# Differential attention on one core: transposes and value products further behind the scores, row products and gated steps at other places

## The chip, the cores and the metric

One core of a Trainium2 chip runs the whole program. The time is device microseconds of one execution; the number before is the median of three runs. An execution's own trace has the profiled times. Engines are called PE (TensorE matmuls), PEld (its weight loads), DVE (VectorE), ACT (ScalarE), POOL (GpSimd) and SP (SyncE, which issues the weight DMAs).

## The reference, cut to what matters

256 tokens of width 1024 pass two transformer layers and a third block (gated linear attention, block attention, a feed-forward of width 4096). The first layer is differential attention: 8 heads with two score maps each over 512 keys (256 of a context, 256 of the tokens).

```python
def diff_softmax_mix(q, k, v, lam):
    s = jnp.einsum('bqhmd,bkhmd->bhmqk', q * (HEAD_DIM ** -0.5), k).astype(jnp.float32)
    p = jax.nn.softmax(s, axis=-1)
    a = p[:, :, 0] - lam * p[:, :, 1]
    return jnp.einsum('bhqk,bkhe->bqhe', a.astype(v.dtype), v)

def diff_head_out(o, subln_g, lam_init, w_o):
    of = o.astype(jnp.float32)
    of = of * lax.rsqrt(jnp.mean(of * of, axis=-1, keepdims=True) + LN_EPS) * subln_g * (1.0 - lam_init)
    return of.astype(o.dtype).reshape(B, Q, V_WIDTH) @ w_o
```

Queries and latent keys get a rotary embedding first. Each layer is modulated by rows computed from a condition vector c (`m = silu(c) @ w_mod + b_mod`, 48 column blocks for each of two layers), and ends in layer norms and a gated feed-forward (`swiglu`).

## The kernel before, in words

**Weights as a stream.** All weights come as 426 blocks of 128 x 1024 fp32 in the order of `make_plan` (L82). `Stream` (L242) keeps 11 raw blocks ahead by DMA (`dma`, L251, on SP's queue). Emitting an item (`emit`, L265) means one of three things. A "w" block is split into a high and a low fp32r part: ACT copies hi (L285), DVE subtracts lo (L291), and a matmul by it is three fp32r matmuls (`mmN` L357, `mmK` L380, `mmK_tail` L394). A few blocks stay raw and are used as fp32 (`get32`); of the output projection WO these are keys 4 to 7. An "m" block is a row product on DVE (L269): a 128 x 1024 block times the condition row, summed into one column of `mc`. Up to 8 split blocks are alive.

**When items are emitted.** `done` (L336) tells that a block is used up, and `pump` (L307) then emits what follows, at most one m a call, unless `hold` is set; `step(n)` (L319) emits up to n items at a given place, but no split beyond 7 alive; `get` and `mods` emit until a given item is there. So the plan's order and these calls place every split and row product in the queues of ACT and DVE, which run in program order.

**K, Q and V.** K is projected first. The loop at L616 does Q in 8 blocks (12 matmuls of 512 columns each) and puts between them the transposes of the roped and plain keys (`k_transposes` L598): kt3 behind Q2, ktc[0] behind Q3, kt2 behind Q5, ktc[1] behind Q6. The rope of a 128 x 1024 tile (L578) is four DVE operations on each half. kt2 is roped on DVE behind Q3's items, from two "mm" PSUM tiles, which the first V projection needs again. `v_proj(0, tt)` (L631) makes the first half of the values in four pieces, with the ropes of q and `st.step(2)` between them; the second half, `v_proj(1, tt)`, lies within the attention loop at rounds VAT = (0, 3, 6, 9).

**The attention loop** (L801). 16 items (token tile t, head h), one a round. Round i issues for item i `at_scores` (L656: two matmuls into one of two "big" PSUM tiles, DVE reduce to the negative maxima at L666, two exponentials on ACT at L667 and L668 with their sums), for item i-1 `at_mix` (L671: reciprocal, a small product, then p0 + coefficient x p1 at L675), for item i-2 `at_tr` (L677: four PE transposes into a "tr" tile, an ACT copy), for item i-3 `at_av` (L686: eight matmul instructions by the values and a square on ACT). After four heads `at_norm` and `at_norm2` normalize the group (DVE, with a power on POOL between), and `tr_half` (L719), five rounds behind the group's last scores, transposes it: ACT writes the high part, DVE the low one, or ACT alone where it stays fp32. `st.step(ATS[i])` emits two items in rounds 0 to 8 and one in rounds 9 to 20. From round 16 on `wo0` (L761) does output rows of the first token tile as WOK lists them. `load_x` and `scale_x` bring the residual and scale it on ACT (L799) in rounds 14 and 15.

**After it.** `linK8` (L914) finishes the output projection with the layer norm of tile 0 inside it; `ffn` (L942) runs six chunks, each with G, U, transposes (`tr`) and O products, the latter one chunk behind. Its `mid` callbacks make rows from columns (`col_row` L767: two sets of four PE transposes, two ACT copies). In the third block `steps` (L1526) places the gated linear attention's small pieces between projections: `g_z`, `g_b`, `g_kl`, `g_qk` and others, by round.

Of the kernel before, what the change touches and what calls it, by code (L numbers as in the profile page):

```python
# [40 lines left out]
NV = 5  # L41
NB = 17
XL = 9
W0 = 4
W1 = 64
# [6 lines left out]
WOK = {0: (0,), 1: (1, 2), 2: (3, 4), 3: (5, 6, 7)}  # L52
ATS = (2,) * 9 + (1,) * 12
VAT = (0, 3, 6, 9)
TK = 2
# [10 lines left out]
VM = (1, 1, 1, 1, 0, 0, 0, 0)  # L66
# [105 lines left out]
def body(ctx: ExitStack, tc: tile.TileContext, wst, prm, cst, cst2, poolp, xT_d, cT_d, x_d, head, lam_d,  # L172
# [443 lines left out]
    for k in range(KD):  # L616
# [5 lines left out]
        if k == 3:  # L622
            kt2 = rope(two(kps[2]), 0)
            k_transposes(ktc[0], 0)
        if k == 5:
            k_transposes(kt2, 2)
        if k == 6:
            k_transposes(ktc[1], 1)
    qr = {}

    def v_proj(c, tt):  # L631
# [5 lines left out]
        mmN(ps, lh, mkey(("V", c), 4))  # L637
        if tt == 3:
            st.hold = c == 1
            st.done(*mkey(("V", c), 4))  # L640
        A.activation(vv[:, tt, c * 512:(c + 1) * 512], ps, AF.Copy)

    for tt in range(4):
        v_proj(0, tt)
        st.step(TK)
        if tt < 2:
            qr[tt] = rope([(qps[tt], 0, 1024)], tt)
        else:
            q_transposes(qr[tt - 2], tt - 2)
    a1.close()  # L650
# [3 lines left out]
    ss, ssum, ops, state, osb, rr = {}, {}, {}, {}, {}, {}  # L654

    def at_scores(t, h):  # L656
        g = (t, h // 4)
        if h % 4 == 0:
            ssum[g] = small(4)
        sm = small(8)  # L660
        pr = [a2.t([P, 512], "p0", bufs=4), a2.t([P, 512], "p1", bufs=2)]
# [4 lines left out]
        V.tensor_reduce(sm[:, 0:2], ps, AX.X, OP.max, negate=True)  # L666
        A.activation(pr[0], ps[:, 0], AF.Exp, bias=sm[:, 0:1], accum_out=ssum[g][:, h % 4:h % 4 + 1])  # L667
        A.activation(pr[1], ps[:, 1], AF.Exp, bias=sm[:, 1:2], accum_out=sm[:, 2:3])  # L668
        state[t, h] = pr, sm, ssum[g][:, h % 4:h % 4 + 1]

    def at_mix(t, h):  # L671
        pr, sm, s0 = state[t, h]
        V.reciprocal(sm[:, 4:5], sm[:, 2:3])
        V.scalar_tensor_tensor(sm[:, 5:6], sm[:, 4:5], nlam, s0, op0=OP.mult, op1=OP.mult)
        V.scalar_tensor_tensor(pr[0], pr[1], sm[:, 5:6], pr[0], op0=OP.mult, op1=OP.add)  # L675

    def at_tr(t, h):  # L677
        pr = state.pop((t, h))[0]
        ps = trt()
        for j in range(4):  # L680
            TE.transpose(ps[:, j * P:(j + 1) * P], pr[0][:, j * P:(j + 1) * P], ident)
        aT = a2.t([P, 512], "aT", bufs=2)
        A.activation(aT, ps, AF.Copy)
        state[t, h] = aT

    def at_av(t, h):  # L686
        aT = state.pop((t, h))
# [1096 lines left out]
```

## Time and profile before

| | |
|---|---|
| median of 3 runs | 1149.41 us (1147.62 to 1149.92) |
| the profiled execution's own time | 1149.09 us |
| its span | 1147.2 us |
| mean granted clock of PE | 0.996 |
| busy share PE, PEld, DVE, ACT | 97%, 77%, 66%, 49% |

Times in the rows count from the span's first instruction. A row's duration for a matmul is modelled and overlaps the next, so the work of PE is read from one start to the next. "[0.98 <-DVE tok L592]" says how long the engine was idle before the row and what ended that.

### The profile page before, as it was taken

What the parts mean: (1) busy time and instruction counts of PE and PEld (TensorE: products, weight loads), DVE (VectorE), ACT (ScalarE), POOL (GpSimd) and SP (SyncE); (2) the same over time, 40 slices, a digit from 0 to 9 for tenths busy, and PEclk for the clock granted to TensorE, in tenths of its full rate; (3) what the DMA queues carried; (4) which work ended last, traced back from release to release, by engine and by line L of the source; (5) the groups of instructions that cost most, each with busy time, mean ns of one, the idle gap of its engine ahead of it and who ended that gap; (6) DMA issues with size and microseconds to landing.
All of it is one profiled execution on the core that took longest, in us unless ns stands there. A gap on an engine that the chain in (4) does not pass through costs nothing.

```text
span 1147.2 us, 14156 instructions
## 1 busy us (share of the span) xinstructions
PE 1110.0 (97%) x5186; PEld 880.4 (77%) x5186; DVE 759.9 (66%) x1114; ACT 557.4 (49%) x913; POOL 22.6 (2%) x35
## 2 busy tenths in 40 slices
PE   7999888999999999999999999999999999999998
PEld 3578665678888776888888688887778877888887
DVE  7984967669986865577455865545636776555465
ACT  3452456454444427534443765557226355445353
POOL 0000000000000000000000110000000000000000
PEclk9999999999999999999999999999999999999999
DMA  9973741569997926568464654553434646464611
GB/s 360 359 261 116 275 147 60 195 233 372 343 419 280 332 79 220 191 215 303 168 225 146 224 196 147 189 193 126 169 108 146 208 147 210 162 212 164 207 38 37
DMA packets 65922, 234.62 MB, mean 205 GB/s; under 512 B 7323, under 2 KB 8347, under 8 KB 65852
## 3 DMA queue, kind: packets, MB, share of 16 engines
q1 hardware_dynamic: 64080, 227.97, 55.9%
q10 hardware_dynamic: 1772, 5.74, 1.5%
q8 instruction: 41, 0.67, 0.2%
q14 instruction: 29, 0.24, 0.1%
HBM read 232.63 MB, written 1.05 MB: 204 GB/s over the span
## 4 chain that ended last, share of the span: by engine, by line
PE 79%; DVE 10%; ACT 4%; issue 3%; DMA 2%; POOL 0%; SPq 0%; ACTq 0%; POOLq 0%; DVEq 0%
PE mm L378 16%; PE mm L376 16%; PE mm L377 16%; PE big L390 12%; PE big L392 6%; DVE lo L291 3%; DMA raw<-in_dram 2%; DVE junkb L526 2%; DVE raw L269 1%; PE big L384 1%; DVE st L666 1%; PE big L404 1%; PE big L405 1%; PE big L403 1%; PE tr L981 1%
## 5 line engine op out<-in xcount | busy, mean ns | idle before, releaser
L291 DVE TENSOR_TENSOR lo<-raw,hi 128x1024 fp32r<-128x1024 f32 x316 | 374.5, 1221 | 133.1 <-ACT hi L285 129.6
L285 ACT ACTIVATE hi<-raw 128x1024 fp32r<-128x1024 f32 x316 | 321.5, 1056 | 70.7 <-PE mm L378 52.2
L376 PE MATMUL mm<-hi,xTh 128*128 128x512 f32 (+1 forms) x872 | 337.6, 387 | 2.8 <-ACT xTh L425 2.7
L377 PE MATMUL mm<-lo,xTh 128*128 128x512 f32 (+1 forms) x872 | 331.8, 380 | 2.0 <-DVE lo L291 1.3
L378 PE MATMUL mm<-hi,xTl 128*128 128x512 f32 (+1 forms) x872 | 332.2, 381 | 0.6 <-DVE xTl L738 0.4
L376 PEld LDWEIGHTS mm<-hi,xTh 128*128 128x128 f32 x872 | 164.1, 188 | 38.4 <-ACT xTh L425 4.6
L378 PEld LDWEIGHTS mm<-hi,xTl 128*128 128x128 f32 x872 | 164.0, 188 | 34.1 <-DVE xTl L426 1.9
L377 PEld LDWEIGHTS mm<-lo,xTh 128*128 128x128 f32 x872 | 164.2, 188 | 33.4 <-DVE lo L291 3.6
L269 DVE SCALAR_TENSOR_TENSOR raw<-raw,crow 128x1024 f32<-128x1024 f32 x80 | 96.8, 1219 | 0.0
L390 PE MATMUL big<-hi,hh 128*128 128x512 f32 x256 | 80.6, 396 | 0.0
L390 PE MATMUL big<-lo,hh 128*128 128x512 f32 x256 | 79.2, 391 | 0.0
L392 PE MATMUL big<-hi,hl 128*128 128x512 f32 x256 | 79.0, 390 | 0.0
L425 ACT ACTIVATE hh<-tr 128x512 fp32r<-128x512 f32 (+1 forms) x40 | 22.9, 575 | 89.6 <-PE tr L981 49.2
L961 ACT ACTIVATE h<-mm 128x512 f32<-128x512 f32 (+1 forms) x24 | 13.5, 561 | 91.6 <-PE mm L378 91.6
L392 PEld LDWEIGHTS big<-hi,hl 128*128 128x128 f32 x256 | 48.0, 188 | 10.3
L390 PEld LDWEIGHTS big<-lo,hh 128*128 128x128 f32 x256 | 48.0, 188 | 10.3
L426 DVE TENSOR_TENSOR hl<-tr,hh 128x512 fp32r<-128x512 f32 (+1 forms) x40 | 26.3, 662 | 44.0 <-ACT hh L425 43.2
L390 PEld LDWEIGHTS big<-hi,hh 128*128 128x128 f32 x256 | 46.7, 188 | 8.6
L420 POOL TENSOR_TENSOR st<-st,half 128x4 f32<-128x4 f32 (+1 forms) x28 | 21.7, 776 | 1029.0 <-DVE st L418 1015.9
L1607 DVE TENSOR_TENSOR h<-h 128x512 f32<-128x512 f32 x16 | 11.0, 689 | 33.8 <-ACT h L1606 33.7
L1606 ACT ACTIVATE h<-mm 128x512 f32<-128x512 f32 x16 | 9.6, 598 | 39.8 <-PE mm L378 39.8
L667 ACT ACTIVATE p<-big,st 128x512 f32<-128x512 f32 x16 | 11.0, 689 | 31.4 <-DVE st L666 31.4
(316 smaller groups left out, 1256.2 us busy)
## 6 DMA issues: line engine op xcount, KB each, us to landing
raw<-in_dram SPq DMA_DIRECT2D x426, 512.0 KB, 5.0
row<-in_dram ACTq DMA_DIRECT2D x8, 512.0 KB, 6.2
tok<-in_dram SPq DMA_DIRECT2D x8, 256.0 KB, 8.0
xa<-in_dram SPq DMA_DIRECT2D x2, 512.0 KB, 6.6
out_dram<-sg SPq DMA_DIRECT2D x3, 256.0 KB, 2.0
pmat<-in_dram ACTq DMA_DIRECT2D x1, 544.0 KB
crow<-in_dram ACTq DMA_DIRECT2D x1, 512.0 KB, 6.4
out_dram<-sg SPq DMA_DIRECT2D x2, 128.0 KB, 1.7
```

What stands on the lines that cost most here:

```text
L269: V.scalar_tensor_tensor(raw, raw, 1.0, crow, op0=OP.mult, op1=OP.mult, accum_out=mc[l][:, nb:nb + 1])
L285: A.activation(hi, raw, AF.Copy)
L291: V.tensor_tensor(lo, raw, hi.bitcast(F32), op=OP.subtract)
L376: TE.matmul(ps, h, hi[:, sl], start=s, stop=False)
L377: TE.matmul(ps, h, lo[:, sl], start=False, stop=False)
L378: TE.matmul(ps, l, hi[:, sl], start=False, stop=e)
L390: TE.matmul(halves[f], h, w[:, f * 512:(f + 1) * 512], start=first and b == 0, stop=False)
L392: TE.matmul(halves[f], l, hi[:, f * 512:(f + 1) * 512], start=False, stop=last)
L420: G.tensor_tensor(r, v, half_e[:, :w], op=OP.pow)
L425: A.activation(dh, ps, AF.Copy)
L426: V.tensor_tensor(dl, ps, dh.bitcast(F32), op=OP.subtract)
L526: V.scalar_tensor_tensor(junk, raws[b], 1.0, crow if s_ else ccrow, op0=OP.mult, op1=OP.mult, accum_out=acc[2 * s_ + b])
```

## The change

In the plan five more row products come ahead of the second half of V (NV, NB, VM), and those woven into the first feed-forward start three blocks later (W0, W1). In the Q loop ktc[0] goes behind Q4, ktc[1] stays behind Q6 and kt2 goes behind the first V projection. The four pieces of V emit 2, 2, 2 and 1 items, behind the rope or the transposes, and the stream is held from the fourth on. In the attention loop the mix, the transposes, the products and the group's steps lie one round further behind the scores; the exponentials are issued behind the transposes of an older item; the small division is done for two heads at once in even rounds; the squares of three groups are one ACT pass and one DVE reduce; gated steps come only in rounds 0, 2, 6, 10, 16, 17 and 18; V and the output rows move. Four further places change behind the loop. Removed bodies that stand above are left out.

```diff
-NV = 5
-NB = 17
+NV = 10
+NB = 12
 XL = 9
-W0 = 4
-W1 = 64
+W0 = 7
+W1 = 67
...
-WOK = {0: (0,), 1: (1, 2), 2: (3, 4), 3: (5, 6, 7)}
-ATS = (2,) * 9 + (1,) * 12
-VAT = (0, 3, 6, 9)
-TK = 2
+WOK = {0: (0, 1), 1: (2, 3), 3: (4, 5, 6, 7)}
+ATS = {0: 3, 2: 4, 6: 4, 10: 4, 16: 2, 17: 7, 18: 1}
+VAT = (0, 2, 6, 10)
+TK = (2, 2, 2, 1)
...
-VM = (1, 1, 1, 1, 0, 0, 0, 0)
+VM = (1, 1, 1, 6, 0, 0, 0, 0)
...
             kt2 = rope(two(kps[2]), 0)
-            k_transposes(ktc[0], 0)
-        if k == 5:
-            k_transposes(kt2, 2)
-        if k == 6:
-            k_transposes(ktc[1], 1)
+        if k in (4, 6):
+            k_transposes(ktc[k // 2 - 2], k // 2 - 2)
...
         mmN(ps, lh, mkey(("V", c), 4))
+        A.activation(vv[:, tt, c * 512:(c + 1) * 512], ps, AF.Copy)
         if tt == 3:
-            st.hold = c == 1
+            st.hold = True
             st.done(*mkey(("V", c), 4))
-        A.activation(vv[:, tt, c * 512:(c + 1) * 512], ps, AF.Copy)
 
     for tt in range(4):
         v_proj(0, tt)
-        st.step(TK)
         if tt < 2:
             qr[tt] = rope([(qps[tt], 0, 1024)], tt)
         else:
             q_transposes(qr[tt - 2], tt - 2)
+        if tt == 0:
+            k_transposes(kt2, 2)
+        st.step(TK[tt])
...
+        V.tensor_reduce(sm[:, 2 * (i % 2):2 * (i % 2) + 2], ps, AX.X, OP.max, negate=True)
+        state[i] = ps
+
+    def at_exp(i):
...
+        pr = [a2.t([P, 512], "p0", bufs=4), a2.t([P, 512], "p1", bufs=3)]
+        A.activation(pr[0], ps[:, 0], AF.Exp, bias=sm[:, 2 * o_:2 * o_ + 1],
+                     accum_out=ssum[t, h // 4][:, h % 4:h % 4 + 1])
+        A.activation(pr[1], ps[:, 1], AF.Exp, bias=sm[:, 2 * o_ + 1:2 * o_ + 2], accum_out=sm[:, 4 + o_:5 + o_])
+        state[i] = pr
+
+    def at_small(i):
+        t, h = items[i]
+        sm = pairs[i // 2]
+        V.reciprocal(sm[:, 6:8], sm[:, 4:6])
+        V.scalar_tensor_tensor(sm[:, 6:8], sm[:, 6:8], nlam, ssum[t, h // 4][:, h % 4:h % 4 + 2],
+                               op0=OP.mult, op1=OP.mult)
+
+    def at_mix(i):
+        pr = state[i]
+        V.scalar_tensor_tensor(pr[0], pr[1], pairs[i // 2][:, 6 + i % 2:7 + i % 2], pr[0], op0=OP.mult, op1=OP.add)
+        state[i] = pr[0]
...
-        jk = a2.t([P, P], "jk", bufs=2)
-        A.activation(jk, ps, AF.Square, accum_out=ss[g][:, h % 4:h % 4 + 1])
+        if g == (1, 1):
+            A.activation(a2.t([P, P], "jk1"), ps, AF.Square, accum_out=ss[g][:, h % 4:h % 4 + 1])
+        elif h % 4 == 3:
+            sq[g] = a2.t([P, 512], "jk")
+            A.activation(sq[g], ops[g], AF.Square)
 
     def at_norm(g):
...
+        v, r = small(4), small(4)
+        if g in sq:
+            V.tensor_reduce(ss[g], sq.pop(g).rearrange("p (h d) -> p h d", d=P), AX.X, OP.add)
+        V.scalar_tensor_tensor(v, ssum[g], LN_EPS, ssum[g], op0=OP.mult, op1=OP.mult)
+        V.scalar_tensor_tensor(v, ss[g], 1.0 / 128, v, op0=OP.mult, op1=OP.add)
+        G.tensor_tensor(r, v, half_e[:, :4], op=OP.pow)
+        rr[g] = r
...
+    def at_half(n):
+        t, f = items[n][0], items[n][1] // 4
+        tr_half(osb[t, f], f, t, xTh, xTl, scalars=sub, f32=f in WOF)
+
+    for i in range(n_it + 4):
+        g5, g6, g7 = [items[i - n] if n <= i < n_it + n and (i - n) % 4 == 3 else None for n in (5, 6, 7)]
+        last = i == n_it + 3
...
+        if i == n_it:
             g1c = mcol(0, 2)
...
         if i < n_it:
+            at_scores(i)
+        if 3 <= i < n_it + 3:
+            at_tr(i - 3)
+        if i < n_it:
+            at_exp(i)
+        if g7:
+            at_half(i - 7)
+        if i >= 4:
+            at_av(i - 4)
+        if i % 2 == 0 and 2 <= i < n_it + 2:
+            at_small(i - 2)
+        if 2 <= i < n_it + 2:
+            at_mix(i - 2)
+        if g6:
+            at_norm2((g6[0], g6[1] // 4))
+        if g5:
+            at_norm((g5[0], g5[1] // 4))
+        if last:
+            at_norm((1, 1))
+        st.step(ATS.get(i, 0))
         for tt in range(4):
             if VAT[tt] == i:
                 v_proj(1, tt)
         if i - n_it in WOK:
             wo0(WOK[i - n_it])
...
+        if i == n_it + 2:
+            col_row(g1c, s[1])
+        if last:
+            at_norm2((1, 1))
+            at_half(n_it - 1)
...
             st.done((name, k))
-        if name == "WO":
-            keep(KW["c"])
+            if name == "WO" and k == 3:
+                st.hold = True
...
-                if (j, 0) in mid:
-                    mid[j, 0]()
                 o(j - 1, 0, False)
-                if (j, 1) in mid:
-                    mid[j, 1]()
...
-            ln_core(t, ps, cur["grow"])
+            ln_core(t, ps, cur["grow"], lambda: st.step(2 * t))
...
     def wo_mid():
         cur["cols"] = mod_cols(0, 1, 0)
-
-    def wo_t0():
         cur["rows"] = ln_rows(0, ALPHA)
-        x_t(0)()
+
+    wo_t0 = x_t(0)
...
     def mid_gbr():
-        nx["G"] = col_row(nx["gb"][0])
+        nx["G"], nx["B"] = col_row(nx["gb"][0]), col_row(nx["gb"][1])
+        cur["grow"] = col_row(nx["g1p"])
         nx["cols"] = mod_cols(1, 1, 2)
-
-    def mid_br():
-        nx["B"] = col_row(nx["gb"][1])
-
-    def mid_pr():
-        cur["grow"] = col_row(nx["g1p"])
...
-    steps = [lambda: (g_z(0), g_z(1)), lambda: (g_b(0), g_b(1)), lambda: (g_kl(0), g_kl(1)), lambda: g_qk(0),
+    steps = [lambda: (g_z(0), g_z(1)), lambda: g_b(0), lambda: (g_b(1), g_kl(0)), lambda: (g_kl(1), g_qk(0)),
              lambda: g_qk(1), lambda: (g_a(0), g_a(1)), lambda: g_kv(0)]
```

## Rows read from the trace of the kernel before

**Rows 1.** The page, part 1: busy time of each engine.

```profile
PE 1110.0 (97%) x5186; PEld 880.4 (77%) x5186; DVE 759.9 (66%) x1114; ACT 557.4 (49%) x913; POOL 22.6 (2%) x35
```

**Rows 2.** Two stretches by windows: length, busy of PE, PEld, DVE, ACT, POOL, granted clock, DMA, GB/s.

```profile
118.00:212.00 94.00, 81.41 (x418) 55.70 (x417) 69.47 (x139) 49.58 (x132) 4.05 (x4) 0.98 0.46 156
83.00:90.00 7.00, 4.65 (x18) 3.73 (x18) 6.93 (x11) 2.14 (x3) 0.00 (x0) 0.76 0.92 355
```

**Rows 3.** What PE's weight loads waited for, 110 to 215: total, times, longest (us).

```profile
PEld tr L681 <- issue: 15.1, 9, 4.5
```

**Rows 4.** Timeline of PE in the Q stage: start, duration (us), engine, line, operation.

```profile
82.55 0.61 PE L392 MATMUL big<-hi,xTl 128*128 128x512 f32 x2
...
86.14 1.08 PE L602 MATMUL tr<-cst,tok 128*128 128x128 f32 x4 [1.36 <-DVE tok L592]
86.88 1.20 PE L390 MATMUL big<-hi,xTh 128*128 128x512 f32 x2
...
89.36 0.62 PE L390 MATMUL big<-hi,xTh 128*128 128x512 f32 x2
```

**Rows 5.** Timeline of DVE in the Q stage: the last step of the rope of kt2.

```profile
85.30 0.69 DVE L592 TENSOR_TENSOR tok<-tok,ropeb 128x512 f32<-128x512 f32 x1
```

**Rows 6.** Timeline of PE in the attention loop.

```profile
117.99 1.13 PE L665 MATMUL big<-kT,qz 64*128 64x512 f32 x4
...
124.71 1.99 PE L665 MATMUL big<-kT,qz 64*128 64x512 f32 x8
128.32 0.63 PE L681 MATMUL tr<-cst,p 128*128 128x128 f32 x4 [1.63 <-issue]
...
151.17 1.06 PE L694 MATMUL mm<-vv,aT 128*128 128x128 f32 x8
152.16 1.13 PE L665 MATMUL big<-kT,qz 64*128 64x512 f32 x4
153.22 0.66 PE L681 MATMUL tr<-cst,p 128*128 128x128 f32 x4
153.71 1.06 PE L694 MATMUL mm<-vv,aT 128*128 128x128 f32 x8
...
159.51 0.63 PE L681 MATMUL tr<-cst,p 128*128 128x128 f32 x4 [3.68 <-DVE st L707]
160.53 1.89 PE L694 MATMUL mm<-vv,aT 128*128 128x128 f32 x8 [0.40 <-ACT jk L696]
...
211.64 0.60 PE L722 MATMUL tr<-cst,osb 128*128 128x128 f32 x4
```

**Rows 7.** Timeline of PE among the output rows.

```profile
198.90 0.62 PE L390 MATMUL big<-hi,xTh 128*128 128x512 f32 x2
...
200.29 0.60 PE L681 MATMUL tr<-cst,p 128*128 128x128 f32 x4
...
206.49 5.32 PE L384 MATMUL big<-raw,pw 128*128 128x512 f32 x12
```

**Rows 8.** Groups of DVE and ACT by line, 118 to 212: count, busy, mean ns, idle before.

```profile
L269 DVE SCALAR_TENSOR_TENSOR raw<-raw,crow 128x1024 f32<-128x1024 f32 x17 | 20.1, 1219 | 0.0
L666 DVE TENSOR_REDUCE st<-big 128x2 f32<-128x1024 f32 x16 | 19.5, 1218 | 0.9 <-PE big L665 0.9
L675 DVE SCALAR_TENSOR_TENSOR p<-p,st,p 128x512 f32<-128x512 f32 x16 | 12.0, 752 | 0.6
...
L667 ACT ACTIVATE p<-big,st 128x512 f32<-128x512 f32 x16 | 11.0, 689 | 31.4 <-DVE st L666 31.4
```

**Rows 9.** Timeline of PE at the end of the first feed-forward layer.

```profile
391.54 1.04 PE L774 MATMUL tr<-cst,Gc 128*128 128x128 f32 x8
...
409.06 0.62 PE L390 MATMUL big<-hi,hh 128*128 128x512 f32 x2
```

**Rows 10.** Timeline of DVE at the same place.

```profile
400.95 0.68 DVE L426 TENSOR_TENSOR hl<-tr,hh 128x512 fp32r<-128x512 f32 x1
```

**Rows 11.** What PE waited for, 770 to 830.

```profile
PE tr L1447 <- DVE la L1442: 1.0, 1, 1.0
```

More of the change, by code (lines that the diff above doesn't have):

```diff
@@ L649, in body, with at_scores @@
             q_transposes(qr[tt - 2], tt - 2)
+        if tt == 0:
+            k_transposes(kt2, 2)
+        st.step(TK[tt])
     a1.close()
     a2 = Pool("a2")
-    ss, ssum, ops, state, osb, rr = {}, {}, {}, {}, {}, {}
-    def at_scores(t, h):
-        g = (t, h // 4)
+    ss, ssum, ops, state, osb, rr, pairs, sq = {}, {}, {}, {}, {}, {}, {}, {}
+    def at_scores(i):
+        t, h = items[i]
         if h % 4 == 0:
-            ssum[g] = small(4)
-        sm = small(8)
-        pr = [a2.t([P, 512], "p0", bufs=4), a2.t([P, 512], "p1", bufs=2)]
+            ssum[t, h // 4] = small(4)
+        if i % 2 == 0:
+            pairs[i // 2] = small(8)
+        sm = pairs[i // 2]
         ps = big().rearrange("p (m k) -> p m k", m=2)
@@ L665, in at_scores, with at_tr, at_av @@
             TE.matmul(ps[:, m], qz[d, h, t * P:(t + 1) * P], kT[d, h, :], start=True, stop=True)
[L666 to L678, printed above, removed]
+        V.tensor_reduce(sm[:, 2 * (i % 2):2 * (i % 2) + 2], ps, AX.X, OP.max, negate=True)
+        state[i] = ps
+    def at_exp(i):
+        t, h = items[i]
+        ps, sm, o_ = state.pop(i), pairs[i // 2], i % 2
+        pr = [a2.t([P, 512], "p0", bufs=4), a2.t([P, 512], "p1", bufs=3)]
[4 more added lines that the diff above has]
+    def at_small(i):
+        t, h = items[i]
+        sm = pairs[i // 2]
+        V.reciprocal(sm[:, 6:8], sm[:, 4:6])
[5 more added lines that the diff above has]
+        state[i] = pr[0]
+    def at_tr(i):
+        p0 = state.pop(i)
         ps = trt()
         for j in range(4):
-            TE.transpose(ps[:, j * P:(j + 1) * P], pr[0][:, j * P:(j + 1) * P], ident)
+            TE.transpose(ps[:, j * P:(j + 1) * P], p0[:, j * P:(j + 1) * P], ident)
         aT = a2.t([P, 512], "aT", bufs=2)
         A.activation(aT, ps, AF.Copy)
-        state[t, h] = aT
-    def at_av(t, h):
-        aT = state.pop((t, h))
+        state[i] = aT
+    def at_av(i):
+        t, h = items[i]
+        aT = state.pop(i)
         g = (t, h // 4)
@@ L799, in scale_x @@
         A.activation(xa[t], xa[t], AF.Copy, scale=ALPHA)
-    for i in range(n_it + 5):
+    def at_half(n):
[4 more added lines that the diff above has]
+        last = i == n_it + 3
         if i == XL:
@@ L823, in body @@
             wo0(WOK[i - n_it])
-        if 2 <= i <= n_it + 1:
-            at_tr(*items[i - 2])
-        st.step(ATS[i])
-        if 3 <= i <= n_it + 2:
-            t, h = items[i - 3]
-            at_av(t, h)
-            if h % 4 == 3:
-                at_norm((t, h // 4))
-        if i >= 5 and items[i - 5][1] % 4 == 3:
-            t, f = items[i - 5][0], items[i - 5][1] // 4
-            tr_half(osb[t, f], f, t, xTh, xTl, scalars=sub, f32=f in WOF)
+        if i == n_it + 2:
[3 more added lines that the diff above has]
+            at_half(n_it - 1)
     st.hold = False
@@ L1149, in ple @@
             A.activation(pw[t][:, f * 512:(f + 1) * 512], pst[f], AF.Copy)
-    ffn(0, fp, x_t(1), ac0(0), mid_pool, ac0(1), {XM: mid_xa, 2: mid_g2c, 3: mid_g2r, 4: mid_gb, 5: mid_gbr, (5, 0): mid_br, (5, 1): mid_pr})
+    ffn(0, fp, x_t(1), ac0(0), mid_pool, ac0(1), {XM: mid_xa, 2: mid_g2c, 3: mid_g2r, 4: mid_gb, 5: mid_gbr})
     pps = [big()]
```

20 lines of the change are left out of this document (1 added, 19 removed).

## Prediction

> **What bounds the kernel now.** I read the page's first part, then the two stretches by windows, then the waits of TensorE's weight loads, then the timelines of TensorE (PE), VectorE (DVE) and ScalarE (ACT) around each edit. PE is recorded busy for 97% of the span [rows 1], so nothing an edit does to DVE or ACT counts unless it fills a hole on PE, and the sum below is a sum of holes. The attention loop is where they are: between 118 and 212 us PE is busy 81.4 of 94.0 us [rows 2], so 12.6 us are idle by record. In the Q stage the stretch 83 to 90 us has 4.65 of 7.0 us busy at a granted clock of 0.76 [rows 2]. The weight loads that wait in the attention are mainly those of L681, the transposes of the mixed scores: 15.1 us in nine waits [rows 3]. They stand in PE's queue two rounds behind their scores and ahead of everything else, and a score has to pass reduce, exponentials and mix on DVE and ACT first.
>
> [...]
>
> **Work in the attention, by the starts of rows.** A value product takes 0.99 us (151.17 to 152.16), a pair of scores 1.06, four transposes 0.49 (153.22 to 153.71), so a round has 2.54 us of PE work [rows 6]; 16 rounds are 40.6. A V projection takes 124.71 - 117.99 less its scores' 1.06 = 5.66; four are 22.6. Output rows: 1.39 us for a split key (198.90 to 200.29), 1.72 for an fp32 one (5.15 for three from 206.49) [rows 6, 7]; four of each are 12.5. Four group transposes and one row from a column (two sets of transposes) are six times 0.49 = 2.9. Sum 78.6 us, against 117.99 to 211.64 + 0.49 = 94.1. So 15.5 us are idle or at the low clock.
>
> **The change, part by part.** All against the profiled execution, 1149.1 us (its span of 1147.2 and 1.9 around it), which is 0.3 us below the median of the runs shown.
>
> *Q stage.* The transposes of kt2 stand between Q5 and Q6. PE finishes Q5 at 82.55 + 0.45 = 83.0 and starts Q6 at 86.88, held by the rope on DVE that ends at 85.99 [rows 4, 5]. Of these 3.9 us the eight transposes are 0.98; 2.9 are waiting. Q6 then runs slowly: 2.48 us from 86.88 to 89.36 where three pairs cost 3 x 0.455 = 1.37 at full clock, 1.1 lost. The change puts these transposes behind the first V projection, 5.66 us of PE work later than now plus Q6 and Q7; the rope doesn't move. So the wait goes whole: **-4.0 us** (bounds -2.9, if the clock falls elsewhere, to -4.0). Late next would be the accumulators that the same rope releases for the first V projection; PE gets there near 89, three us after the rope's end. The other k transposes only change places among ready ones. Three row products move from behind V's blocks into Q5 to Q7, where DVE has nothing that PE awaits, and the V1 blocks are split after the second q rope; their first reader is the projection behind the first scores, some ten us later.
>
> *Attention.* The loop goes from mix at one round, transposes at two and products at three behind the scores to two, three and four; the gated steps go from one or two in every round to bursts ahead of the V projections (3, 4, 4, 4) and of the output rows; the small divisions are done for two heads at once; the squares for three of four groups in one ACT pass and one DVE reduce. DVE's prices: reduce 1.22, mix 0.75, row product 1.22 [rows 8], some 0.08 less from start to start; a split I take like a row product, one pass over a tile of the same size. DVE has about 2.0 us a round for scores, less than PE's 2.54, so without bursts PE leads. In a V round PE has 8.2 us and DVE 2.0 + 4 x 1.14 = 6.6. Before, 17 row products lay in this stretch [rows 8] and six more queued just ahead of the first reduce; now 14 do. I walked through the rounds with these prices, each engine in its queue order. What is left: round 4, transposes wait 1.5 us, since round 3's reduce and mix queue behind the burst of round 2; round 10 0.5, the transposes of the first head whose mix follows a group's norm; round 12 1.0, after round 10's burst, which also holds the low half of the transposed group; round 15 3.0, where ACT does a scale of x before each of two copies, the high half of the group's transposes comes behind the exponentials, its low half blocks DVE, and the pair's division and mix stand behind that. Sum 6.0; I add 0.8 for hand-overs. Of 15.5 us 6.8 stay: **-8.7 us**. Bounds: all gone -15.5; none +0 (the lockstep rival goes beyond). The burst ahead of the output rows lies beside 8 split and fp32 keys of matmuls; the last group's norm lies beside four fp32 keys (6.9 us), where before only three were left.
>
> *New waits, clock.* A wait of about 3 us costs more than itself: after the 3.7 us wait at 159.51 the product took 1.89 us by record against 1.06, and the Q stage above lost 1.1 at the lower clock. After 1.63 us at 128.32 the transposes took 0.63, as unhindered ones (0.66) [rows 6]. I expect two new waits of 3 us (round 15 and the one below) and take half of 1.1 for each: **+1.1** (0 to +2.2).
>
> *Feed-forward tail of the first layer.* Three rows are made from columns in one place instead of three, and eight row products start three blocks later. DVE had seven items between the last U and the low half of the first transposes (hl), which started at 400.95 [rows 10]; by the new plan there are ten, one of them the last O block, so hl starts 3 x 1.14 = 3.4 later and is ready at 405.0. On PE: from 391.54 [rows 9] seven sets of transposes at 0.49 (ACT's copies as fast, an estimate), 395.0; the first O product, 24 matmuls as in a V projection, 5.6, 400.6; transposes 0.5; then the last O product, whose third matmul needs hl: 3.5 us of waiting, then 22 of 24 matmuls, 5.0, end 410.0 against 409.06: **+1.0** (bounds -2.5, DVE not late, to +1.0).
>
> *GLA.* g_b(1) no longer follows g_b(0) at once; the wait of 1.0 us on la goes [rows 11], and one of the later sets may wait for a PSUM slot: **-0.7** (0 to -1.0).
>
> *At nothing.* The hold at the third output row and the step inside the normalization change no order: rows 4 to 7 are fp32 and release no slot, and at the step the splits stand at their limit. The two row loads move ahead of the normalization on ACT's queue; PE has the whole second half of the output product there, and if that cover were gone it would be a fraction of a us. Two row products leave that place for later ones in a stretch where DVE isn't awaited.
>
> Sum: -4.0 - 8.7 + 1.1 + 1.0 - 0.7 = -11.3, so **1137.8 us**.
>
> **Rivals.**
> *The waits nearly all go.* ACT and DVE keep up and 2 us stay: 4.8 less, 1.1 of clock less, 1131.9. For it: PE work exceeds DVE's in every kind of round. Against: bursts of four on an engine with one queue.
> *DVE still sets the pace.* Each burst and each group's norm puts the chain one step back and 11.5 us stay: 4.7 more, 1142.5. For it: DVE is busy 69.5 of 94 us now [rows 2], and 80 us would hold almost as much.
> *Every wait brings the low clock.* If all four of my residual waits were followed by 1.1 us of loss, 3.3 more, 1141.1. For it: the slow product behind 159.51; against it the one behind 128.32 [rows 6]. [...]
> *The Q wait only moves*, to the first V projection: 4.0 more, 1141.8. The rope's end at 85.99 speaks against it.
> *Lockstep, slower than before.* In every pair of rounds DVE's division waits for the second head's exponentials on ACT, and next round's reduce, from which the next exponentials come, stands behind it. A pair then costs two reduces, one set of exponentials, the division, two mixes and a pair of scores: 2.44 + 1.45 + 0.45 + 1.5 + 1.06 = 6.9 [rows 6, 8] (0.45 and 1.45 are estimates, from two small operations and from L667 twice), where PE needs 5.1. Eight pairs add 14.4 to the 6.8: the attention loses 5.7 instead of winning 8.7, 1152.2. It turns slower from 6.5 us a pair. Against it: the exponentials of a head run while DVE does the next reduce, so the loop without the scores and one reduce is 4.6.
>
> **How the numbers follow.** Forecast 0.58; waits nearly gone 0.17; DVE sets the pace 0.13; clock 0.04; Q wait moves 0.04; lockstep 0.04. A measurement of this kernel tells about 0.2%, 2.3 us. All but lockstep lie faster by more than that; the far bounds of the second rival (15.5 us stay, a late tail) end within it, for 0.04. So faster 0.92, same 0.04, slower 0.04. The range goes from 1129 (beyond the waits that go, toward the bounds, which give 1149.1 - 4.0 - 15.5 - 2.5 - 1.0 = 1126.1) to 1145 (13 us staying in the attention and the bad end of the clock).
>
> **What would show it.** Right: no PE wait on the k rope before Q6 and full clock in Q6; the attention from first scores to last group transposes in 85 to 86 us; its waits on L681 down to some 6 us, the largest near the scale of x; about 3 us of waiting on hl in the last O product; no wait on la. Wrong: waits of 1 us or more in every second round (lockstep); the first V projection held; PE waiting on lo blocks in the feed-forward, where I cost the later row products at nothing.

## The result, and the profile after

The changed kernel takes 1139.44 us (median of 5 runs, 1137.78 to 1142.11) against 1149.41 before (5 runs): ratio 0.9917, 95% interval 0.9903 to 0.993. The prediction was 1137.8 us, its range 1129 to 1145. The profiled execution has 1138.74 us and a span of 1136.8, 10.4 less than before.

Page, part 1, of the changed kernel, against [rows 1]:

```profile
PE 1107.6 (97%) x5186; PEld 878.9 (77%) x5186; DVE 757.2 (67%) x1089; ACT 556.5 (49%) x892; POOL 23.7 (2%) x35
```

TensorE's busy share is 97% as before; nothing in it shows 10 us of gain.

Windows of the changed kernel over the same work as [rows 2]: the attention, and the Q stage at the place of the former wait.

```profile
113.00:198.00 85.00, 79.71 (x431) 55.70 (x430) 66.12 (x110) 51.12 (x114) 5.09 (x4) 1.00 0.44 152
79.00:86.00 7.00, 7.00 (x36) 5.85 (x36) 6.93 (x13) 1.09 (x2) 0.00 (x0) 1.00 0.99 387
```

The Q stretch is now wholly busy at full clock (4.65 of 7.00 at 0.76 before); the attention has 5.3 us of recorded idle where it had 12.6. What weight loads and transposes of the mixed scores wait for, 110 to 215 (L694 is the former L681, [rows 3]):

```profile
PEld tr L694 <- issue: 9.8, 9, 3.7
```

The prediction's sign was "down to some 6 us", from 15.1; by this row it missed. On PE itself the rows of that line show 4.9 us of idle time behind the mix.

Timeline of PE in the changed kernel, from the Q stage to the last group transposes ([rows 4, 6]):

```profile
82.94 0.62 PE L392 MATMUL big<-hi,xTl 128*128 128x512 f32 x2
83.39 0.61 PE L390 MATMUL big<-hi,xTh 128*128 128x512 f32 x2
...
114.28 1.13 PE L665 MATMUL big<-kT,qz 64*128 64x512 f32 x4
...
132.56 0.66 PE L694 MATMUL tr<-cst,p 128*128 128x128 f32 x4 [1.20 <-DVE p L687]
...
165.50 0.63 PE L694 MATMUL tr<-cst,p 128*128 128x128 f32 x4 [0.86 <-DVE p L687]
...
172.46 1.13 PE L665 MATMUL big<-kT,qz 64*128 64x512 f32 x4
176.47 0.63 PE L694 MATMUL tr<-cst,p 128*128 128x128 f32 x4 [2.88 <-DVE p L687]
176.94 1.06 PE L708 MATMUL mm<-vv,aT 128*128 128x128 f32 x8
178.27 0.63 PE L694 MATMUL tr<-cst,p 128*128 128x128 f32 x4 [0.27 <-DVE mcol L803]
...
196.86 0.60 PE L739 MATMUL tr<-cst,osb 128*128 128x128 f32 x4
```

Q6 follows Q5 without a gap (83.39). First scores come at 114.28 instead of 117.99, the last group transposes at 196.86 instead of 211.64: the attention takes 196.86 + 0.49 - 114.28 = 83.1 us, 11.1 less. Three waits over 0.5 us are left, in rounds 4, 12 and 15. (For the first three groups the steps lie two rounds further behind the group's last scores than before, not one as said ahead of the prediction: `at_norm`, `at_norm2` and `at_half` come at five, six and seven rounds, where they came at three, four and five.)

Where the time went, by the **lag** (start of a PE instruction after, less the start of the same one before): +0.4 ahead of Q (the first weights of the program), then -4.1 in the Q stage, -11.1 in the attention (lag -14.8 at its end), and from there it is given back: +1.0 between 254 and 289 us of the kernel before, +1.3 at the end of the first feed-forward, +1.6 between 437 and 457 (a low clock, see below), +0.4 around the gated linear attention. Sum -10.5; at the end the lag is -10.4. ("By the lag" and a lag in us always mean this shift; the longer lag, or the lag alone, is the number of rounds by which mix, transposes and products follow their scores.)

The 1.0 us in the middle of the feed-forward come with weight loads of PE that wait for a split's low half. From 235 to 300 us, in the kernel before:

```profile
PEld mm L377 <- DVE lo L291: 0.2, 1, 0.2
```

In the changed kernel:

```profile
PEld mm L377 <- DVE lo L291: 1.2, 2, 0.7
```

The end of the first feed-forward in the changed kernel, the timeline of PE ([rows 9]):

```profile
377.81 1.04 PE L791 MATMUL tr<-cst,Gc 128*128 128x128 f32 x8
...
391.51 0.50 PE L405 MATMUL big<-hi,hl 128*128 128x512 f32 x1 [2.66 <-DVE hl L426]
...
396.63 0.62 PE L390 MATMUL big<-hi,hh 128*128 128x512 f32 x2
```

DVE at the same place ([rows 10]):

```profile
388.87 1.21 DVE L269 SCALAR_TENSOR_TENSOR raw<-raw,crow 128x1024 f32<-128x1024 f32 x1
...
390.77 1.28 DVE L426 TENSOR_TENSOR hl<-tr,hh 128x512 fp32r<-128x512 f32 x2
```

hl is late behind a queue of splits and row products; 18.8 us from the first row's transposes to the next weights, where it was 17.5. The +1.6 comes with no new wait. The window behind a wait of 1.82 us in the kernel before:

```profile
442.00:448.00 6.00, 5.80 (x24) 4.50 (x25) 3.96 (x6) 5.42 (x10) 0.00 (x0) 1.00 0.85 288
```

The window behind the same wait, of the same length, in the changed kernel:

```profile
430.00:436.00 6.00, 5.81 (x19) 4.41 (x18) 3.53 (x5) 5.43 (x9) 0.00 (x0) 0.72 0.79 296
```

The granted clock is 1.00 in the one and 0.72 in the other. This is read from one execution of each kernel; whether the change brings it is not shown (see the last section).

### The profile page after: what moved, and what is told of

Same layout as the page of the kernel before. It is cut to its first block, busy times and chain, and to the rows that moved or that the text cites. A ratio compares the mean times of both kernels' runs of the same rounds, so it can differ in the third digit from the quotient of the medians.

```text
span 1136.8 us, 14098 instructions
## 1 busy us (share of the span) xinstructions
PE 1107.6 (97%) x5186; PEld 878.9 (77%) x5186; DVE 757.2 (67%) x1089; ACT 556.5 (49%) x892; POOL 23.7 (2%) x35
## 4 chain that ended last, share of the span: by engine, by line
PE 78%; DVE 12%; ACT 4%; issue 3%; DMA 3%; POOL 0%; SPq 0%; ACTq 0%; POOLq 0%; DVEq 0%
PE mm L378 15%; PE mm L377 15%; PE mm L376 15%; PE big L390 12%; PE big L392 6%; DVE lo L291 3%; DVE junkb L526 2%; DMA raw<-in_dram 2%; DVE raw L269 2%; PE big L384 1%; PE big L405 1%; DVE st L666 1%; PE big L403 1%; PE big L404 1%; PE tr L1008 1%
## 5 line engine op out<-in xcount | busy, mean ns | idle before, releaser
L392 PEld LDWEIGHTS big<-hi,hl 128*128 128x128 f32 x256 | 48.1, 188 | 10.4
L420 POOL TENSOR_TENSOR st<-st,half 128x1 f32<-128x1 f32 (+1 forms) x24 | 17.7, 739 | 830.9 <-DVE st L418 830.9
L996 DVE TENSOR_TENSOR h<-h,mm 128x512 f32<-128x512 f32 (+1 forms) x24 | 15.4, 640 | 16.8 <-PE mm L378 16.8
```

Source lines behind the costliest of these rows:

```text
L392: TE.matmul(halves[f], l, hi[:, f * 512:(f + 1) * 512], start=False, stop=last)
L420: G.tensor_tensor(r, v, half_e[:, :w], op=OP.pow)
```

## The experiments

"Attention" is, as above, first scores to the end of the last group transposes: 94.1 us before, 83.1 changed.

**The Q edit alone**, on the kernel before.

```diff
-            k_transposes(ktc[0], 0)
-        if k == 5:
-            k_transposes(kt2, 2)
+        if k == 4:
+            k_transposes(ktc[0], 0)
...
+        if tt == 0:
+            k_transposes(kt2, 2)
```

> The kernel before with one edit: the transposes of kt2 behind the first V projection, those of ktc[0] one place later. Theory (the wait for the rope ahead of Q6 goes whole and comes back nowhere): first scores 4.0 us earlier (113.9 to 114.4 instead of 117.99), the rest of the kernel shifted by that, so 1145.1 us, ratio 0.9965. Rival (the wait only moves to the first V projection, whose accumulators the same rope releases): 1149 us, ratio 1.000, and a wait of some 3 us ahead of the first V matmul. In both theories the attention keeps its 94.1 us.

Measured 1146.42 us, 0.9971 (0.9961 to 0.9982). PE in its Q stage and at the first scores:

```profile
82.53 0.62 PE L392 MATMUL big<-hi,xTl 128*128 128x512 f32 x2
82.98 0.62 PE L390 MATMUL big<-hi,xTh 128*128 128x512 f32 x2
...
113.87 1.13 PE L666 MATMUL big<-kT,qz 64*128 64x512 f32 x4
```

First scores 4.1 us earlier, nothing waits ahead of V, and the lag stays at -4.1 through the attention and up to 775 us. The wait was removed, not moved. At the end the lag is only -2.9: a wait of 0.70 us in the third block, far from the edit, is followed by a low clock that costs 1.6 us; the wait on la just behind it goes and gives 1.2 back. PE there, and the window behind it with a granted clock of 0.58:

```profile
775.08 1.95 PE L1438 MATMUL tr<-w2b,gst 33*128 33x512 f32 x4 [0.70 <-issue]
```

```profile
778.00:782.00 4.00, 4.00 (x12) 3.14 (x11) 0.69 (x1) 3.94 (x6) 0.00 (x0) 0.58 0.01 4
```

**The lag without the bursts**, on the changed kernel. All else that the change does in the loop stays: the paired divisions, the squares in one pass, the later exponentials, the new places of V and of the output rows.

```diff
-ATS = {0: 3, 2: 4, 6: 4, 10: 4, 16: 2, 17: 7, 18: 1}
+ATS = {i: 2 if i < 9 else 1 for i in range(20)}
```

> The changed kernel with the longer lag kept and the bursts undone: two gated steps in each of the rounds 0 to 8, one in every later one. Theory of the prediction (DVE is what is short where a round has no V projection, so the row products belong ahead of V projections): in rounds 3 to 5 and 7 to 8 DVE has 4.3 us a round against 2.54 on TensorE, the slack of one round is used up, 4 to 5 us of the attention come back: attention 87 to 88 us instead of 83.1, 1143 us, ratio 0.995. Rival (the lag alone does it): attention within 1.5 us of 83.1, 1139 to 1140.5 us, ratio 0.992.

Measured 1149.92 us, 1.0003 (0.9994 to 1.0013), attention 93.7. Both expectations fall: the longer lag without the bursts gives 0.4 us of 11. One of the reasons is seen on DVE of this kernel, and on ACT, whose high half of the split comes behind the exponentials and a square:

```profile
150.18 0.74 DVE L687 SCALAR_TENSOR_TENSOR p<-p,st,p 128x512 f32<-128x512 f32 x1
153.21 1.23 DVE L291 TENSOR_TENSOR lo<-raw,hi 128x1024 fp32r<-128x1024 f32 x1 [2.29 <-ACT hi L285]
154.35 1.22 DVE L666 TENSOR_REDUCE st<-big 128x2 f32<-128x1024 f32 x1
```

```profile
152.12 1.06 ACT L285 ACTIVATE hi<-raw 128x1024 fp32r<-128x1024 f32 x1
```

PE of the same kernel just after it:

```profile
156.83 0.63 PE L694 MATMUL tr<-cst,p 128*128 128x128 f32 x4 [2.76 <-DVE p L687]
157.29 1.43 PE L708 MATMUL mm<-vv,aT 128*128 128x128 f32 x8
158.66 2.08 PE L665 MATMUL big<-kT,qz 64*128 64x512 f32 x4
```

A split's low half stands at the head of DVE's queue, idle, for 2.29 us, because its high half stands on ACT behind exponentials; reduce and mix behind it are late and PE waits 2.76. The scores after it take 2.08 instead of 1.13, by my reading at a lower clock (0.95 on average over the whole attention). The same pattern comes again at 177, with a granted clock of 0.72 from 176 to 182; the wait of 2.74 at 187 is the one that the changed kernel has in round 15. In the earlier rounds DVE is simply full, as its window shows (third busy number):

```profile
132.00:140.00 8.00, 5.83 (x30) 4.18 (x32) 7.93 (x15) 3.49 (x10) 0.00 (x0) 0.83 0.74 239
```

**The bursts without the lag**, on the kernel before.

```diff
-ATS = (2,) * 9 + (1,) * 12
-VAT = (0, 3, 6, 9)
+ATS = (3, 0, 4, 0, 0, 0, 4, 0, 0, 0, 4, 0, 0, 0, 0, 0, 2, 7, 1, 0, 0)
+VAT = (0, 2, 6, 10)
```

> The kernel before with its lag of two and three rounds and only the places of gated steps and V projections as in the changed kernel (3, 4, 4, 4 ahead of the V projections in rounds 0, 2, 6, 10; 2, 7, 1 at the end). Theory (the short lag is the cause: a score needs reduce 1.2, exponentials 1.45, division 0.45 and mix 0.75 within two rounds of 2.54 less the scores themselves, so each round waits with or without steps in it): the attention wins 3 us at most, 91 to 94 us, 1146 to 1149 us. Rival (the row products between the scores' work are the cause and the bursts alone remove it): the attention wins 7 us or more, 87 us or less, 1142 us, ratio 0.994.

Measured 1145.08 us, 0.996 (0.9948 to 0.9973); the attention takes 90.6, a gain of 3.5. Its longest wait is longer than any of the kernel before (3.68):

```profile
174.39 1.08 PE L681 MATMUL tr<-cst,p 128*128 128x128 f32 x4 [4.95 <-DVE st L707]
```

Another 1.3 us lie in the Q stage: the wait for the rope is there (4.67 of 7.00 us busy from 83 to 90), but the granted clock is 1.00 instead of 0.76. No edit of this run lies in that stage.

So of the attention's 11 us the lag with its other edits gives 0.4, the bursts with the new places of V 3.5, and some 7 come only with both. Neither run takes out the paired divisions or the squares alone, so what each of these adds is not shown. The whole attention by windows (length, busy PE, PEld, DVE, ACT, POOL, granted clock, DMA, GB/s) before, with the lag alone, with the bursts alone, and in the changed kernel:

```profile
117.99:212.13 94.14, 81.55 (x418) 55.84 (x418) 69.61 (x139) 49.59 (x132) 4.05 (x4) 0.98 0.46 156
114.34:208.04 93.70, 82.43 (x418) 56.55 (x418) 63.59 (x102) 48.99 (x111) 5.34 (x4) 0.95 0.39 129
116.46:207.04 90.58, 82.10 (x418) 56.19 (x418) 69.64 (x139) 50.13 (x132) 4.05 (x4) 0.96 0.46 162
114.28:197.35 83.07, 77.78 (x418) 54.20 (x418) 65.50 (x109) 49.85 (x112) 5.09 (x4) 1.00 0.44 152
```

Idle time is 12.6, 11.3, 8.5 and 5.3 us: of the 7 us that come only with both, 1.9 are idle time. The other 5 are the same instructions taking longer in the runs without both, in part at the low clock (0.95 and 0.96 on average), which the changed kernel's attention (1.00) does not have. How much of this is owed to the shorter waits, and how much to chance (the last section), is not shown.

**The spread steps ahead of the exponentials**, on the kernel with spread steps.

```diff
+        st.step(ATS.get(i, 0))
         if i < n_it:
             at_exp(i)
...
-        st.step(ATS.get(i, 0))
```

> The kernel with the longer lag and gated steps spread over the rounds (attention 93.7 us), with one more edit: the steps stand ahead of the round's exponentials instead of at the round's end. Theory (the spread steps cost so much because DVE's low half of a split waits for ACT's high half, which stands behind exponentials and the squares: 2.3 us of idle DVE twice, ahead of the reduce, each followed by a TensorE wait of 2.8 us): with the high half ahead of the exponentials these waits shrink and the attention takes 87 to 90 us, 1143 to 1146 us. Rival (DVE is short of time in rounds without a V projection, 4.3 us of work against 2.54): the attention stays at 92 us or more, 1148 to 1150 us.

Measured 1149.85 us, 1.0006, attention 94.1. DVE's idle times for a high half shrink from 2.29 to 0.99 and the two waits of 2.76 to 1.75, as the theory says, but others grow: in rounds 3 to 5 they sum to 3.9 us where they were 2.7 (2.35 at 133), and 0.8 us is new in round 13. So the time is the rival's. Both causes are at work, DVE full in the early rounds and the hand-over in the later ones. That the bursts help because they put both beside V projections fits these rows, but is argued and not tested by itself.

**The row products of the feed-forward at their old place**, on the changed kernel.

```diff
-W0 = 7
-W1 = 67
+W0 = 4
+W1 = 64
```

> The changed kernel with the eight row products in the first layer's feed-forward at their old place, three blocks earlier (W0 = 4, W1 = 64). Theory (their later place makes TensorE wait for split blocks between 254 and 289 us, 1.0 us, and puts hl of the last O product behind more items on DVE, a wait of 2.66 us that cost 1.3): 1.0 to 2.4 us come back, 1136.3 to 1137.7 us, ratio 0.989 to 0.990, the wait on hl under 1 us. Rival (the hl wait comes from the three rows made ahead of the O products, whose copies TensorE and the queue share, and the waits on lo blocks from the attention's earlier end against the weights' arrival): nothing comes back, 1138.5 to 1139.5 us, the wait on hl 2 us or more.

Measured 1135.83 us, 0.9878 (0.9864 to 0.9891). By the lag against the changed kernel 1.0 us comes back in the middle of the feed-forward and 1.9 at its end. The wait on hl is gone; what is left in the last O product is a wait that the kernel before has too (0.62 us):

```profile
390.21 0.49 PE L404 MATMUL big<-lo,hh 128*128 128x512 f32 x1 [0.57 <-DVE lo L291]
```

DVE has seven items ahead of hl again (three row products and four splits, where the changed kernel has five of each); the three rows made in one place stay, with 0.8 us of small waits for their copies, where the kernel before has 0.9 at its rows. More came back than expected, and the end of the feed-forward is now 0.6 us shorter than before.

**Scaling of x two rounds later, and the old grouping of the linear attention's steps.**

```diff
-        if i == XL + 5 or i == XL + 6:
-            scale_x(i - XL - 5)
+        if i == XL + 7 or i == XL + 8:
+            scale_x(i - XL - 7)
...
-lambda: g_b(0), lambda: (g_b(1), g_kl(0)), lambda: (g_kl(1), g_qk(0)),
+lambda: (g_b(0), g_b(1)), lambda: (g_kl(0), g_kl(1)), lambda: g_qk(0),
```

> The changed kernel with two edits that lie 600 us apart and are read each in its own stage: the two scalings of x in rounds 16 and 17 instead of 14 and 15, and the gated-linear-attention steps in their old grouping. Scaling: the prediction named ACT's scaling of x as what makes TensorE wait in round 15 (2.88 us). Theory now (the scaling delays the exponentials by only 0.4 us, since they wait for the reduce anyway): the wait falls to 2.2 to 2.5 us. Rival (the prediction's reading): the wait falls by 1.0 us or more. GLA: by the trace of the changed kernel the regrouping took the wait on la away and put others of the same size in its place, so the old grouping changes the lag by 0.3 us at most; the prediction's term would make it 0.7 us slower there. Together 1138 to 1140 us, ratio 0.991 to 0.993.

Measured 1138.82 us, 0.9913 (0.9898 to 0.9928). The old grouping is 0.38 faster by the lag than the changed kernel's. The wait in round 15 falls by 0.38, from 2.88 to 2.50, but the rows behind it are slower here (transposes 0.99 and products 1.92 us, where the changed kernel has 0.63 and 1.06), which I read as the low clock, and the attention comes out at 83.9. PE of this kernel:

```profile
175.96 0.99 PE L694 MATMUL tr<-cst,p 128*128 128x128 f32 x4 [2.50 <-DVE p L687]
176.74 1.92 PE L708 MATMUL mm<-vv,aT 128*128 128x128 f32 x8
```

**The half of the group transposes behind the mix.**

```diff
-        if g7:
-            at_half(i - 7)
         if i >= 4:
             at_av(i - 4)
...
             at_mix(i - 2)
+        if g7:
+            at_half(i - 7)
```

> The changed kernel with the half of the group transposes (its TensorE transposes, ACT's high half and DVE's low half) emitted behind the round's products, division and mix instead of ahead of them. Theory (the 2.88 us wait in round 15 is DVE's queue standing 2.5 us behind the low half, which waits for ACT's high half, which waits behind the exponentials; division and mix behind it need nothing new): the wait goes to under 0.5 us, attention 83.1 to 80.5 us, 1136.5 to 1137 us, ratio 0.989. Rival (the block only moves one instruction on and now holds the next round's reduce, so that the next exponentials and mix are late): TensorE waits as long one round later, attention 82.5 to 83.5 us, ratio 0.9915.

The place it acts on, on DVE of the changed kernel:

```profile
170.78 1.21 DVE L666 TENSOR_REDUCE st<-big 128x2 f32<-128x1024 f32 x1
174.46 0.75 DVE L429 SCALAR_TENSOR_TENSOR xTl<-tr,subc,xTh 128x512 fp32r<-128x512 f32 x1 [2.48 <-ACT xTh L428]
...
175.58 0.75 DVE L687 SCALAR_TENSOR_TENSOR p<-p,st,p 128x512 f32<-128x512 f32 x1
```

Measured 1138.58 us, 0.9913 (0.9899 to 0.9927), attention 83.4. The waits of rounds 12 and 15 go (0.86 and 2.88), but one of 2.25 comes at the transposes of round 16: the low half now holds the next reduce. DVE of this kernel:

```profile
173.00 0.75 DVE L429 SCALAR_TENSOR_TENSOR xTl<-tr,subc,xTh 128x512 fp32r<-128x512 f32 x1 [1.36 <-ACT xTh L428]
173.66 1.22 DVE L666 TENSOR_REDUCE st<-big 128x2 f32<-128x1024 f32 x1
```

And the low clock follows the wait. PE of this kernel (the named mcol is a small operation just behind the mix):

```profile
175.68 0.63 PE L694 MATMUL tr<-cst,p 128*128 128x128 f32 x4 [2.25 <-DVE mcol L803]
176.15 1.36 PE L708 MATMUL mm<-vv,aT 128*128 128x128 f32 x8
```

The window behind it, at a granted clock of 0.59:

```profile
176.00:180.00 4.00, 4.00 (x18) 3.42 (x17) 3.01 (x7) 2.65 (x7) 1.01 (x1) 0.59 0.02 4
```

**The last three edits on the attention and the feed-forward together** (old W0 and W1, later scaling, half behind the mix).

```diff
-W0 = 7
-W1 = 67
+W0 = 4
+W1 = 64
...
-        if i == XL + 5 or i == XL + 6:
-            scale_x(i - XL - 5)
+        if i == XL + 7 or i == XL + 8:
+            scale_x(i - XL - 7)
...
-        if g7:
-            at_half(i - 7)
...
             at_mix(i - 2)
+        if g7:
+            at_half(i - 7)
```

> The changed kernel with the row products of the first layer's feed-forward at their old place, the scalings of x in rounds 16 and 17, and the half of the group transposes behind the mix. The three act in different places, so if each does what its theory says the gains add: 3.3 (measured for the first) plus 2.5 plus 0.4 from 1139.4 us gives 1133 us, ratio 0.9857. If the block of DVE only moves to the next round, 1135.5 to 1136 us, ratio 0.988.

Measured 1132.79 us, 0.9859 (0.9846 to 0.9873), as the sum of the gains. Not for the expected reason, and by luck: 1.87 us of wait stay in round 16 (attention 81.4, where 80.2 would be the sum), and 1.6 us came from the stretch behind 430, whose clock is 1.00 here and which no edit touches.

**That half one round later for all groups**, on the kernel of the three edits (g7 now counts eight rounds).

```diff
-for n in (5, 6, 7)]
+for n in (5, 6, 8)]
...
-            at_half(i - 7)
+            at_half(i - 8)
```

> The kernel of the three edits (row products of the first feed-forward at their old place, scalings of x in rounds 16 and 17, the half of the group transposes behind the mix; 1132.8 us, attention 81.4) with that half one round later still, behind the mix of round 15 instead of round 14. Theory (the wait of 1.87 us left in round 16's transposes is the reduce and mix of round 15 standing behind DVE's low half of round 14; in round 16 there is no reduce any more): the wait goes to 0.3 us or less, attention 79.6 to 80.0 us, 1131 us, ratio 0.984. Rival (the output rows of round 16 now wait for the low half, which is made just ahead of them): a wait of 1 to 2 us at the first output row in its place, attention 81 to 82 us, 1132.5 us, ratio 0.9855.

Measured 1134.5 us, 0.9867 (0.9853 to 0.9882). The two intervals overlap; the attention, 82.3, is 0.9 us slower, and for neither reason named. The wait of round 16 is gone and one of 0.27 stands in round 15, but the first group's half now lies in round 11, where no V projection covers it, and PE waits 1.48 in round 13; 0.9 more is lost where the third group's half moved into the last round. PE of this kernel:

```profile
168.28 0.63 PE L694 MATMUL tr<-cst,p 128*128 128x128 f32 x4 [1.48 <-DVE p L687]
...
173.78 0.63 PE L694 MATMUL tr<-cst,p 128*128 128x128 f32 x4 [0.27 <-DVE p L687]
```

**One gated step from round 2 to round 0**, on the kernel of the three edits.

```diff
-ATS = {0: 3, 2: 4, 6: 4, 10: 4, 16: 2, 17: 7, 18: 1}
+ATS = {0: 4, 2: 3, 6: 4, 10: 4, 16: 2, 17: 7, 18: 1}
```

> The kernel of the three edits with one gated step moved from the burst of round 2 to that of round 0 (4 and 3 instead of 3 and 4). Theory (the 1.20 us wait of the transposes in round 4 is round 3's reduce and mix standing behind the four row products of round 2, 125.4 to 130.0 us): one row product fewer there but 0.5 us of it given back by a later reduce in round 1, the wait falls to 0.5 to 0.7 us, 1132.2 us, ratio 0.985. Rival (the wait only moves to the transposes of round 3 or stays, since DVE has the same work before it): the sum of the waits in rounds 3 and 4 stays at 1.1 to 1.3 us, 1132.8 us, ratio 0.986.

Measured 1131.75 us, 0.985 (0.9832 to 0.9868); the wait of round 4 falls from 1.20 to 0.85, attention 81.1 for 81.4. The direction is the theory's, the size about half of it. The times of the two kernels overlap, so this is read from the stage alone.

**Both.**

```diff
-for n in (5, 6, 7)]
+for n in (5, 6, 8)]
...
-            at_half(i - 7)
+            at_half(i - 8)
...
-ATS = {0: 3, 2: 4, 6: 4, 10: 4, 16: 2, 17: 7, 18: 1}
+ATS = {0: 4, 2: 3, 6: 4, 10: 4, 16: 2, 17: 7, 18: 1}
```

> Both edits on the kernel of the three: if both theories hold, no wait over 0.7 us in the attention, 78.9 to 79.4 us against 78.6 us of work by the prediction's count, 1130.5 us, ratio 0.9835; if neither, 1132.8 us, ratio 0.986.

Measured 1134.94 us, 0.9868 (0.9853 to 0.9882): the gain of the one and the loss of the other (attention 82.0), and in the profiled execution the low clock behind 425 again (0.61 in the four us from 425.51; 1.5 us lost).

**The half one round later for the second group alone**, with the bursts of 4 and 3 and the three edits.

```diff
-        if g7:
-            at_half(i - 7)
+        if i in (10, 15, 18):
+            at_half({10: 3, 15: 7, 18: 11}[i])
```

> The kernel of the three edits with the bursts of 4 and 3 (1131.75 us, attention 81.07) and the half of the transposed groups one round later for the second group alone, behind the mix of round 15. Theory (one round later takes the 1.87 us wait away at the second group; it lost time only at the first group, where no V projection covers the next round, 1.48, and at the third, 0.8): no wait over 0.9 us in the attention, 79.3 to 79.8 us, 1130.0 to 1130.5 us, ratio 0.983 to 0.984. Rival (DVE's division and mix of round 16 now stand behind the low half, and the next transposes or output rows wait instead): attention 80.5 to 81.5 us, 1131.5 us, ratio 0.985.

Measured 1130.86 us (1130.31 to 1132.47), 0.9843 (0.9829 to 0.9856): faster than the kernel before and the changed one. Against the kernel that it was made from (1131.75) the times overlap; the attention is 1.5 us shorter. PE of this kernel, the two largest waits of the attention apart from 0.34 at a row, and its end:

```profile
131.62 0.66 PE L694 MATMUL tr<-cst,p 128*128 128x128 f32 x4 [0.85 <-DVE p L687]
...
171.60 0.63 PE L694 MATMUL tr<-cst,p 128*128 128x128 f32 x4 [0.26 <-DVE p L687]
...
192.81 0.60 PE L739 MATMUL tr<-cst,osb 128*128 128x128 f32 x4
```

Attention 79.6 us, against 78.6 of work by the prediction's count: almost all of the 15.5 us is gone. The row at 171.60 is round 15's; round 13, where moving all groups had put a wait of 1.48, has none with the first group's half back beside a V projection.

## Why the prediction was right, and where its terms were off

| term | predicted | measured in the changed kernel's profiled execution, by the lag |
|---|---|---|
| Q stage | -4.0 | -4.1 |
| attention | -8.7 | -11.1 |
| low clock behind new waits | +1.1 | 0 there; +1.6 behind an old wait |
| later row products in the feed-forward | 0 | +1.0 |
| end of the first feed-forward | +1.0 | +1.3 |
| linear attention | -0.7 | +0.4 |
| noise ahead of Q | - | +0.4 |
| sum | -11.3 | -10.5 |

That the two sums lie 0.8 us apart is in part luck: the attention came out 2.4 us better than its term, the other terms together 3.2 us worse.

**Right: the Q stage.** The edit alone gives its 4.1 us; the rope's end at 85.99 was the argument and it held. Some 1.3 of the 4.1 are the low clock behind the wait (0.76 from 83 to 90). The run with the bursts without the lag has the same wait, a clock of 1.00 and not this loss, so the part that is sure is 2.8 us, close to the bound of -2.9 that the prediction gave for it.

**Right in mechanism, too small: the attention.** The walk through the rounds named rounds 4, 12 and 15 with 1.5, 1.0 and 3.0 us; they are 1.20, 0.86 and 2.88. What did not come is round 10 (0.5), most of the 0.8 for hand-overs, and the 78.6 us of work were a little too many (77.8 busy at full clock). The mechanism is shown as far as the experiments go: without the bursts the gain is 0.4. For round 15 the step named a chain: scaling, high half behind the exponentials, low half blocking DVE, division and mix behind that. The runs sort it: the scaling is 0.38 of it; the rest is the low half at the head of DVE's queue: moving that half by one step moved the wait to round 16, by one round more took it away.

**Wrong without harm: "a split I take like a row product".** Its own time on DVE is the same (1.22), but it can hold DVE idle 2.3 us for its high half. In the changed kernel bursts put it beside V projections; with spread steps it cost PE 2.76 us at a time. The prediction had no number for what the bursts add to the lag; its theory, put as an expectation for the run without bursts, gave 4 to 5 us for them where 10.6 were measured.

**Wrong in place: the clock.** For two new waits the prediction says "take half of 1.1 for each". They came, with 2.88 and 2.66 us, and the clock behind them stayed at 1.00; it fell, to 0.72 from 430 to 436, behind the 1.82 us wait that the kernel before has too, at 1.6 us, in this execution. That the term and the loss are of like size is chance.

**Wrong: "Two row products leave that place for later ones in a stretch where DVE isn't awaited", and with them the eight of the feed-forward.** Putting the eight back gave 1.0 us in the middle of the feed-forward, where split blocks had come late. The step overlooked that TensorE waits for splits there, though the section on what would show it wrong named the place.

**Right: the end of the feed-forward.** Ten items instead of seven stand ahead of hl, and with seven the wait is gone. Waits and dearer transposes at the rows, which were not counted (0.67 us of waits), came out of the wait on hl, 2.66 for 3.5, and not on top. +1.3 for +1.0 is hl 0.2 us later and 5.1 us of products behind it for 5.0.

**Wrong in sign: the linear attention.** The wait on la (0.98) went, and waits of 0.28, 0.58 and 0.25 at neighbouring transposes came; the old grouping, with the wait on la back, is 0.38 faster.

None of the rivals took place as a whole; the last sign of being wrong, PE waiting on lo blocks in the feed-forward, did. "The waits nearly all go" came true in the last experiment, by edits that the change did not make.

## What to carry to other kernels

A longer software lag and a regrouping of side work can be worth little apart and much together, as here (0.4 and 3.5 us apart, 11 together, part of it the clock): the lag helps little while side items stand in front of the chain it is meant to cover. In this kernel an operation whose first half is on another engine's queue cost least where the long work of a third engine covered the hand-over (the first group's half: no wait in round 13 when beside a V projection, 1.48 us when one round later), and its price elsewhere was that wait (up to 2.5 us on DVE), not its own duration (0.75 for a low half of the transposes, 1.22 for one of a split). A block moved behind the instruction it delayed held the next one here (2.25 us in round 16 for 2.88 in round 15): look one round further before moving it, and at each group's round by itself.

## What the runs showed of the hardware

The low clock behind a wait of TensorE is not told by the length of the wait. In the 14 profiles (before, changed, 12 experiments) 38 rows of PE later than 50 us have 1.5 us or more of idle time ahead of them; in the four us from 17 of them the mean granted clock is between 0.50 and 0.73, from the other 21 it is 1.00. A wait of 3.68 us in the kernel before (0.66 behind it) and one of 4.95 in the run of the bursts were followed by it, and three of 2.7 to 2.9 in the changed kernel (1.00 behind both of its two) and the one with the old row products were not; one of 0.70 in the run of the Q edit (0.58) was. The same 1.82 us wait behind the pooled section was followed by it in 5 of 14 (0.70 in the changed kernel, 0.61 in the run of both edits), though no edit lies near it. Where the lag shows its price, a drop cost 1.3 us (the Q stage before), 1.5 (the run of both edits) and 1.6 (the changed kernel, and the run of the Q edit). What decides it is open: nothing here varied the work ahead of one fixed wait. It need not be the edits, since executions of one kernel differ too. Of the four of the kernel with the bursts of 4 and 3, three took 1131.62 to 1131.84 us at a mean granted clock of 0.999 or more and one 1134.12 at 0.995. So a single profile can show some 1.6 us gained or lost at a place that no edit touches, and a gain of 1 to 2 us is read from its own stage and not from the total.
